# Products of the modulation vectors on VectorE alone and in a pinned order, and the out-projection's first input split at fixed places of the scan

## The chip, the core and the metric

The kernel runs on one core of a Trainium2 chip. The core's engines each work through their own list of instructions in order and wait for each other on semaphores: TensorE (PE: matmuls, with PEld for its weight loads), VectorE (DVE), ScalarE (ACT), GpSimd (POOL) and SyncE (SP), which here issues all the transfers (DMAs). The metric is the time of one execution in microseconds; lower is better.

## The reference, cut to what matters

A sequence of 1024 tokens of width 1024 runs through one Mamba-2 layer and one stick-breaking attention layer. A conditioning vector `c` gives shift, scale and gate vectors for each layer ("modulation"). All is float32.

```python
c_act = silu(c)
shift, scale, gate = split(c_act @ ada_w[0] + ada_b[0], 3)
h = rmsnorm(x) * (1 + scale) + shift
zxbcdt = h @ in_w                      # 2048 z, 2048 x, 4*128 B, 4*128 C, 32 dt
xbc = silu(causal_dwconv(xbc))         # 24 tiles of 128 channels, 4 taps each
y = chunked_scan(x, dt, B, C)          # 4 groups x 8 chunks of 128 tokens
y = group_rmsnorm((y + D * x) * silu(z))
x = x + gate * (y @ out_w)             # the out-projection
# shared K/V with its own shift and scale (c_act @ kv_ada_w), then attention
```

## The kernel before, in words

Every large matmul is made of three: weights and activations are split into a high and a low part, `hi = cast(v)` on ScalarE and `lo = v - hi` on VectorE, and the products hi·hi, hi·lo and lo·hi are summed (`mm3`, L128 to L131). All data are held with channels on the 128 partitions, and the sequence is worked in two halves of 512 tokens.

The program has these stages.

- **Start** (to about 77 us in the profile): input norm, the first two modulation vectors, the first three tiles of the x/B/C projection.
- **Projection and convolution** (77 to 313 us): 21 more tiles. For each, 48 matmuls fill a PSUM tile `pr` of 3 buffers; `conv` then does the first tap on ScalarE (L351) and three taps on VectorE (L353, tile `cv`), a SiLU on ScalarE, and a store to DRAM (`xs_d`, L357). The next tile's weights are split by L123 and L124 (`hx`, `lx`). After some tiles `ada_rest(i)` computes one of the six remaining modulation vectors: eight rows `ar` of 512 KB are loaded (3 buffers) and each is multiplied with the row `crow` and summed. Six of eight products are one VectorE instruction (L369); every fourth (`ADAP = 4`) is a GpSimd product (L366) and a summing pass on ScalarE (L367). The results are needed only by the out-projection and later.
- **Scan** (313 to 640 us): units i = 0 to 7, which are the 4 groups of the first half of the sequence and then of the second; four chunks of 128 tokens each. `chunk_a` loads and exponentiates the decay matrix `lm` (L509, GpSimd L515, ScalarE L518), transposes the chunk into `px` and `pb` (PE L523 to L526, from `xg`, `bt` and `ct`), and multiplies on VectorE (L529 to L539). `chunk_b` does the chunk's matmuls (`yd`, `yo`, `ps`, L550 to L565) and adds up (L562 to L573). `gate` (L575) multiplies with SiLU(z) and sums squares (`sq`: ScalarE L587 and L590, GpSimd L591); `norm_store` of a unit stands two chunks into the next unit and begins with the matmul `rs` of `sq` (L599). The matmuls of the next unit's z projection (`pz`) fill PE between these. PE's order in the scan is written by hand.
- **Out-projection** (from 599 us): `load_y(0)` brings the first half of the scan's output back from DRAM in 16 tiles `yr` (3 buffers, L662) and splits each (`yh` on ScalarE L663, `yl` on VectorE L664). These have no fixed place: outside a hand-written section a scheduler orders each engine's list by its own estimate. For the first half, matmuls `po` of the out-projection are also placed between the last chunks of the scan.
- K/V projection, attention and the last projection follow; nothing there is changed.

`tc.keep_in_program_order(i)` keeps an instruction at its place in the written program on its engine; without it the scheduler may move it ahead.

Of the kernel before, what the change touches and what calls it, by code (L numbers as in the profile page):

```python
# [12 lines left out]
F32 = mybir.dt.float32  # L13
F32R = mybir.dt.float32r
AF = mybir.ActivationFunctionType
ALU = mybir.AluOpType
# [3 lines left out]
P = 128  # L20
# [4 lines left out]
HT = T // NH  # L25
# [6 lines left out]
LAG = 3  # L32
AVD = 1
NPRE = 5
ADAP = 4

VEC = {}
_o = 0
# [9 lines left out]
def f(ap):  # L48
    return ap.bitcast(F32)
# [3 lines left out]
def tile_trunk(ctx, tc, xT, xN, c, vec, ada0, adar, wxbc, wwave, wdt, wz, wmo, wk, wv, wq, wqz, wso, out):  # L53
    nc = tc.nc
    V, S, Q, E, Y = nc.vector, nc.scalar, nc.gpsimd, nc.tensor, nc.sync

    def pool(es, name, bufs=1, **kw):
        return es.enter_context(tc.tile_pool(name=name, bufs=bufs, reuse_waits="tile", **kw))
# [11 lines left out]
    def vv(n, i=None, m=1):  # L70
        o, w = VEC[n]
        if i is None:
            return vt[:, o:o + w]
        return vt[:, o + i:o + i + m]
# [4 lines left out]
    ys_d = [[tc.dram_tile([4, P, HT], F32, name=f"ys_d{g}_{hf}") for hf in range(NH)] for g in range(G)]  # L79
# [14 lines left out]
    def weight_pools(es, n, nr, nw):  # L94
        wp["r"] = pool(es, f"wraw{n}", bufs=nr)
        wp["h"] = pool(es, f"whp{n}", bufs=nw)
        wp["l"] = pool(es, f"wlp{n}", bufs=nw)

    esw = ctx.enter_context(ExitStack())
    weight_pools(esw, 0, 2, 2)  # L100
    esy = esw.enter_context(ExitStack())
    pdt = pool(esy, "pdtv")

    dtv, wdv, acv, eev, nac = [pdt.tile([P, NC_, 32], F32, name=n)
# [5 lines left out]
    def act_tile(name):  # L110
        return act.tile([P, HT], F32R, tag="a", name=name)
# [46 lines left out]
    with ExitStack() as es:  # L158
        pp = pool(es, "pp1", bufs=3, space=PSUM)
        pcr = pool(es, "pcr")  # L160
        crow = pcr.tile([P, D], F32, name="crow")
# [198 lines left out]
        def ada_rest(i):  # L360
            dst = mod[:, (GA0, KSH, KSC, SH1, SC1, GA1)[i], :]
            for d in range(ND):
                r = pada.tile([P, D], F32, tag="ar", name=f"ar{i}_{d}", bufs=3)
                Y.dma_start(out=r, in_=adar[i, d])
                if d % ADAP == ADAP - 1:
                    Q.tensor_tensor(out=r, in0=r, in1=crow, op=ALU.mult)  # L366
                    S.activation(r, r, AF.Identity, accum_out=dst[:, d:d + 1])  # L367
                else:
                    V.scalar_tensor_tensor(out=r, in0=r, scalar=1.0, in1=crow, op0=ALU.mult,  # L369
                                           op1=ALU.mult, accum_out=dst[:, d:d + 1])  # L370
            bn, gn = ((GA0, "b_ga0", None), (KSH, "b_kvsh", None), (KSC, "b_kvsc", "gkv"),
                      (SH1, "b_sh1", None), (SC1, "b_sc1", "g1"), (GA1, "b_ga1", None))[i][1:]
            if gn is None:
                V.tensor_tensor(out=dst, in0=dst, in1=vv(bn), op=ALU.add)
            else:
                V.scalar_tensor_tensor(out=dst, in0=dst, scalar=1.0, in1=vv(bn), op0=ALU.add,
                                       op1=ALU.add)
                V.tensor_tensor(out=dst, in0=dst, in1=vv(gn), op=ALU.mult)
# [83 lines left out]

    pyr = pool(esy, "pyr", bufs=3)
    pxa = pool(esy, "pxa")
    with ExitStack() as es:
        ms = es.enter_context(ExitStack())
        ms.enter_context(tc.manual_schedule(engines={mybir.EngineType.PE}))
# [6 lines left out]
        def zproj(g, hf, j, dst):  # L476
            wh, wl = load_w(wz[4 * g + j], f"z{g}_{hf}_{j}")
            ps = mm_tile(f"pz{g}_{hf}_{j}")
            for k in range(ND):
                mm3(ps, wh[:, k, :], wl[:, k, :], *h0[k][hf], k == 0, k == ND - 1)  # L480
                if k == ND - 1:
                    S.copy(dst, ps)
                yield

        def load_g(g, hf):
            n = f"{g}_{hf}"
            hs = slice(hf * HT, (hf + 1) * HT)
            xg = pw.tile([P, 4, HT], F32, tag="xg", name="xg" + n)
            Y.dma_start(out=xg, in_=xs_d[g][0:4, :, hs].rearrange("j p t -> p j t"))
            bt = pq.tile([P, HT], F32, tag="bt", name="bt" + n, bufs=1)  # L490
            Y.dma_start(out=bt, in_=xs_d[g][4, :, hs])
            ct = pq.tile([P, HT], F32, tag="ct", name="ct" + n)
            Y.dma_start(out=ct, in_=xs_d[g][5, :, hs])
            sz = pw.tile([P, 4, HT], F32, tag="sz", name="sz" + n)
            y = py.tile([P, 4, HT], F32, tag="y", name="y" + n)
            return dict(g=g, hf=hf, xg=xg, bt=bt, ct=ct, sz=sz, y=y)
# [118 lines left out]
        for n, (i, cc) in enumerate(todo):  # L615
            u = units[i]
            c = u["hf"] * CPH + cc
            if cc == 0 and i + 1 < 2 * G:
                units.append(load_g((i + 1) % G, (i + 1) // G))
            z = iter(())  # L620
            if i + 1 < 2 * G:
                v = units[i + 1]
                z = zproj(v["g"], v["hf"], cc, v["sz"][:, cc, :])
            for _ in range(3):
                next(z, None)
            cur = stage
            if n + 1 < len(todo):
                i2, c2 = todo[n + 1]
                nxt = units[i2], units[i2]["hf"] * CPH + c2
                stage = chunk_a(*nxt)  # L630
            for _ in range(3):
                next(z, None)
            if cc == 2 and i > 0:
                norm_store(units[i - 1], sq)
            chunk_b(u, c, *cur)
            for _ in z:
                pass
            if cc == CPH - 1:
                sq = gate(u, n == len(todo) - 1)
        ms.close()  # L640
# [3 lines left out]
    with ExitStack() as es:  # L644
# [8 lines left out]
        def load_y(hf):  # L653
            hs = slice(hf * HT, (hf + 1) * HT)
            yy = []
            for k in range(16):
                mk = b_tile if hf == 1 and k < 8 else act_tile
                yy.append((mk(f"yh{k}_{hf}"), mk(f"yl{k}_{hf}")))
            for k in range(16):
                hi, lo = yy[k]  # L660
                r = pyr.tile([P, HT], F32, tag="yr", name=f"yr{k}_{hf}")
                Y.dma_start(out=r, in_=ys_d[k // 4][hf][k % 4])  # L662
                S.copy(hi, r)  # L663
                V.tensor_tensor(out=lo, in0=r, in1=f(hi), op=ALU.subtract)  # L664
            return yy
# [2 lines left out]
        hk = [[None] * NH for _ in range(ND)]  # L668
        h1 = [[None] * NH for _ in range(ND)]
        rb = [None] * NH  # L670
        ynext = load_y(0)
        for hf in range(NH):
            hs = slice(hf * HT, (hf + 1) * HT)
            yy = ynext
# [1 line left out]
            for d in range(ND):  # L676
# [4 lines left out]
                for kh in range(2):  # L681
                    wh, wl = load_w(wmo[kh, d], f"o{d}_{hf}_{kh}")
                    for k in range(8):
                        mm3(ps, wh[:, k, :], wl[:, k, :], *yy[kh * 8 + k], kh + k == 0, kh * 8 + k == 15)
                V.scalar_tensor_tensor(out=x1[d][hf], in0=ps, scalar=mod[:, GA0, d:d + 1], in1=xr,
                                       op0=ALU.mult, op1=ALU.add)
# [7 lines left out]
            if hf == 0:  # L694
                ynext = load_y(1)
# [16 lines left out]
        for hf in range(NH):  # L712
# [12 lines left out]
            for ch in range(2):  # L725
                ps = [pp.tile([P, 512], F32, tag=f"v{s}", name=f"pv{s}_{ch}_{hf}") for s in range(4)]
                for kp in range(4):
                    wh, wl = load_w(wv[ch, kp], f"v{kp}_{ch}_{hf}", (2, 512))
                    for kk in range(2):
                        k = kp * 2 + kk  # L730
# [222 lines left out]
    with ExitStack() as es:  # L953
# [25 lines left out]
        for hf, c0, c1, ds in ((1, 0, 512, (0, 5, 1, 2, 3, 4, 6, 7)), (0, 0, 256, (6, 7, 0, 1, 2, 3, 4, 5)),  # L979
# [55 lines left out]
            r = pf.tile(sh, F32, tag="rb", name="rb2_" + n)  # L1035
            inv_rms(pss, r, pf.tile(sh, F32, tag="sq", name="rt2_" + n), D)
            done = finish(hf, c0, c1, ds, x2, r)
        for eng, i0, i1 in ((V, 0, 2), (V, 2, 5), (V, 5, 8)):
            m = i1 - i0
            eng.tensor_tensor(out=x2t[:, i0:i1, :], in0=x2t[:, i0:i1, :],  # L1040
                              in1=r.unsqueeze(1).to_broadcast([P, m, w]), op=ALU.mult)
            Y.dma_start(out=out[ds[i0]:ds[i0] + m, :, c0:c1].rearrange("d p t -> p d t"),
                        in_=x2t[:, i0:i1, :])
# [68 lines left out]
```

## Time and profile before

| | |
|---|---|
| median of 3 runs | 1459.53 us (1458.59 to 1461.04) |
| the profiled execution, its own time | 1462.46 us |
| span of its instructions in the profile | 1460.8 us |
| PE busy | 1430.3 us, 98% of the span |
| VectorE, ScalarE, GpSimd busy | 962.0, 736.2, 516.5 us |
| mean granted TensorE clock | 0.994 of full speed |

Times in the profile count from the first instruction; the profiled execution took 1.7 us more than its span. A group of rows may give an engine's idle time and, after an arrow, the instruction or the transfer that ended it.

### The profile page before, as it was taken

To read this page: it belongs to the slowest core of one execution; us is meant where nothing else is said; L and a number is where in the kernel's file an instruction comes from. 1 tells how busy PE (TensorE), PEld (TensorE's weight loads), DVE (VectorE), ACT (ScalarE), POOL (GpSimd) and SP (SyncE) were. 2 spreads that over 40 slices of the span, in tenths; PEclk is the share of its full clock that TensorE was granted. 3 is DMA by queue.
4 is the path that set the end of the run, shared out by engine and by line. 5 is a ranking of instruction groups with operands and counts; after the bars stand their busy time and mean duration, and the time that the engine had idled before them with its cause. 6 is when DMAs were issued, how large, how long until landed. Compare 5 with 4: busy or idle time off the path is not lost.

```text
span 1460.8 us, 20961 instructions
## 1 busy us (share of the span) xinstructions
PE 1430.3 (98%) x7772; PEld 1125.7 (77%) x7772; DVE 962.0 (66%) x1211; ACT 736.2 (50%) x1236; POOL 516.5 (35%) x601
## 2 busy tenths in 40 slices
PE   7998999999999999999999999999999999999997
PEld 4777888887777777778888888887777777777797
DVE  5699975455788887975733627516666666667674
ACT  6654533246666666733532424335555555556452
POOL 0021220002555555531011000027666666667531
PEclk9999999999999999999999999999999999999999
DMA  9358875233577766667433546460222122212253
GB/s 368 129 202 318 295 285 182 101 107 132 183 236 220 234 217 217 195 201 266 151 123 128 182 144 227 159 211 31 80 69 70 59 73 63 68 58 81 92 183 116
DMA packets 105446, 235.76 MB, mean 161 GB/s; under 512 B 9344, under 2 KB 40832, under 8 KB 103296
## 3 DMA queue, kind: packets, MB, share of 16 engines
q1 hardware_dynamic: 105344, 234.42, 47.8%
q8 instruction: 61, 1.00, 0.3%
q14 instruction: 41, 0.34, 0.1%
HBM read 188.51 MB, written 45.88 MB: 160 GB/s over the span
## 4 chain that ended last, share of the span: by engine, by line
PE 90%; DVE 5%; ACT 2%; issue 1%; DMA 1%; POOL 0%; SPq 0%; DVEq 0%; ACTq 0%; POOLq 0%
PE av L891 5%; PE pr L129 5%; PE pr L130 5%; PE pr L131 5%; PE sc L838 4%; PE at L870 4%; PE pz L129 4%; PE pz L131 4%; PE pz L130 4%; PE po L131 4%; PE po L130 4%; PE po L129 4%; PE pq L129 2%; PE pqz L129 2%; PE yd L550 2%; PE pq L131 2%
## 5 line engine op out<-in xcount | busy, mean ns | idle before, releaser
L861 POOL TENSOR_TENSOR be<-be,kp 128x1024 f32<-128x1024 f32 (+2 forms) x96 | 163.3, 1702 | 82.6 <-DVE kp L855 73.6
L841 ACT ACTIVATE kp<-sc 128x1024 f32<-128x1024 f32 (+2 forms) x96 | 75.5, 813 | 149.2 <-PE sc L838 111.3
L855 DVE TENSOR_TENSOR_SCAN kp<-kp,pone 128x128 f32<-128x128 f32 (+3 forms) x128 | 96.7, 803 | 63.8 <-POOL kp L848 63.8
L129 PE MATMUL pr<-h0h,hx 128*128 128x512 f32 x336 | 131.7, 392 | 3.8 <-DVE cv L353 3.8
L131 PE MATMUL pr<-h0h,lx 128*128 128x512 f32 x336 | 131.5, 391 | 0.0
L130 PE MATMUL pr<-h0l,hx 128*128 128x512 f32 x336 | 131.5, 391 | 0.0
L129 PE MATMUL pz<-h0h,hz 128*128 128x512 f32 x256 | 113.0, 441 | 0.0
L130 PE MATMUL po<-yl,ho 128*128 128x512 f32 x256 | 100.9, 394 | 0.6 <-DVE yl L664 0.6
L131 PE MATMUL po<-yh,lo 128*128 128x512 f32 x256 | 100.0, 391 | 1.3 <-DVE lo L124 1.3
L131 PE MATMUL pz<-h0h,lz 128*128 128x512 f32 x256 | 100.4, 392 | 0.0
L130 PE MATMUL pz<-h0l,hz 128*128 128x512 f32 x256 | 100.0, 391 | 0.0
L129 PE MATMUL po<-yh,ho 128*128 128x512 f32 x256 | 100.0, 391 | 0.0
L366 POOL TENSOR_TENSOR ar<-ar,crow 128x1024 f32<-128x1024 f32 x12 | 31.1, 2596 | 182.4 <-DMA ar<-adar 163.0
L518 ACT ACTIVATE lm<-lm,nac 128x128 f32<-128x128 f32 x256 | 78.9, 390 | 31.8 <-POOL lm L515 31.8
L855 DVE TENSOR_TENSOR_SCAN kp<-kp,ab,pone 128x512 f32<-128x512 f32 x64 | 78.3, 1265 | 24.7 <-ACT kp L841 14.2
L124 POOL TENSOR_TENSOR lq<-rq,hq 128x256 fp32r<-128x256 f32 x32 | 22.5, 738 | 177.8 <-ACT hq L123 177.8
L515 POOL TENSOR_SCALAR_AFFINE_SELECT lm<-lm 128x1024 f32<-128x1024 f32 x32 | 42.1, 1316 | 118.3 <-DMA lm<-ac_d 108.9
L555 POOL TENSOR_TENSOR sd<-st,eev 128x512 f32<-128x512 f32 x24 | 37.5, 1561 | 126.1 <-ACT st L567 114.2
L353 DVE SCALAR_TENSOR_TENSOR cv<-pr,vt,cv 128x1023 f32<-128x1023 f32 (+2 forms) x63 | 80.2, 1276 | 0.9
L129 PEld LDWEIGHTS pr<-h0h,hx 128*128 128x128 f32 x336 | 63.5, 189 | 17.4 <-issue 4.2
L123 ACT CAST ho<-ro 128x1024 fp32r<-128x1024 f32 x32 | 33.6, 1052 | 84.5 <-PE po L130 74.3
L870 PEld LDWEIGHTS at<-ident,be 128*128 128x128 f32 x576 | 67.2, 140 | 10.6 <-DVE aT L880 0.9
(258 smaller groups left out, 3886.7 us busy)
## 6 DMA issues: line engine op xcount, KB each, us to landing
ar<-adar SPq DMA_DIRECT2D x48, 512.0 KB, 5.3
lm<-ac_d SPq DMA_DIRECT2D x32, 512.0 KB, 5.0
rz<-wz SPq DMA_DIRECT2D x32, 512.0 KB, 3.8
ro<-wmo SPq DMA_DIRECT2D x32, 512.0 KB, 3.7
xs_d<-sv SPq DMA_DIRECT2D x24, 512.0 KB, 4.1
rx<-wxbc SPq DMA_DIRECT2D x21, 512.0 KB, 4.6
a<-ada SPq DMA_DIRECT2D x8, 1024.0 KB, 10.1
xg<-xs_d SPq DMA_DIRECT2D x8, 1024.0 KB, 6.1
```

Source lines behind the costliest of these rows:

```text
L129: E.matmul(ps, wh, xh, start=first, stop=False)
L130: E.matmul(ps, wh, xl, start=False, stop=False)
L131: E.matmul(ps, wl, xh, start=False, stop=last)
L353: V.scalar_tensor_tensor(out=ac[:, i:], in0=ps[:, :T - i], scalar=vv("cw", m * 4 + 3 - i), in1=ac[:, i:], op0=ALU.mult, op1=ALU.add)
L515: Q.affine_select(out=lm, in_=lm, pattern=[[0, HPG], [1, P]], compare_op=ALU.is_ge, fill=-1e30, base=0, channel_multiplier=-1)
L518: e = S.activation(lm[:, h, :], lm[:, h, :], AF.Exp, bias=nac[:, c, h0_ + h:h0_ + h + 1])
L838: E.matmul(ps[:, a, o:o + w], q[hsl[a], x, i * P:(i + 1) * P], kd[hsl[a], y, HT * c:HT * c + w], start=b == 0, stop=b == 2)
L841: S.activation(kp[:, :, ok:ok + w], ps[:, :, o:o + w], AF.Sigmoid, scale=-0.125)
L855: V.tensor_tensor_scan(out=ka, data0=ka, data1=pone.to_broadcast([P, w]), initial=1.0 if top else above[p, i][:, a, 0:1], op0=ALU.mult, op ...
L861: Q.tensor_tensor(out=be[:, :, o:o + w], in0=be[:, :, o:o + w], in1=kp[:, :, ok + 1:ok + w + 1], op=ALU.mult)
L870: E.transpose(ps[:, j, :], be[:, a, j * P:(j + 1) * P], ident)
L891: E.matmul(ps[hsl[a], cs], vd[:, j, hsl[a]], at[j // 4][:, a, j % 4, cs], start=j == 0, stop=j == nj - 1)
```

## The change

The constant `ADAP` goes. All eight products of a modulation vector are VectorE instructions, and each is kept in program order, behind the taps of the tile that `ada_rest` follows. The pool of the `yr` tiles is made at the beginning of the program. The first half's loads and splits move from `load_y(0)` into the scan's loop: three loads after the first chunk of unit 4, then one split (with the load of the tile three further on) after each chunk of units 5 and 6 and two after each chunk of unit 7, casts and subtractions kept in program order.

```diff
@@ ada_rest
-                if d % ADAP == ADAP - 1:
-                    Q.tensor_tensor(out=r, in0=r, in1=crow, op=ALU.mult)
-                    S.activation(r, r, AF.Identity, accum_out=dst[:, d:d + 1])
-                else:
-                    V.scalar_tensor_tensor(out=r, in0=r, scalar=1.0, in1=crow, op0=ALU.mult,
+                v = V.scalar_tensor_tensor(out=r, in0=r, scalar=1.0, in1=crow, op0=ALU.mult,
                                            op1=ALU.mult, accum_out=dst[:, d:d + 1])
+                tc.keep_in_program_order(v)
@@ before the scan (the pool pyr moves up to the other pools of the first stages)
-    pyr = pool(esy, "pyr", bufs=3)
     pxa = pool(esy, "pxa")
+    y0, yraw = [], []
+
+    def y0_load(k):
+        r = pyr.tile([P, HT], F32, tag="yr", name=f"yr{k}_0")
+        Y.dma_start(out=r, in_=ys_d[k // 4][0][k % 4])
+        yraw.append(r)
+
+    def y0_split():
+        k = len(y0)
+        hi, lo = act_tile(f"yh{k}_0"), act_tile(f"yl{k}_0")
+        tc.keep_in_program_order(S.copy(hi, yraw[k]))
+        tc.keep_in_program_order(V.tensor_tensor(out=lo, in0=yraw[k], in1=f(hi), op=ALU.subtract))
+        y0.append((hi, lo))
+        if len(yraw) < 16:
+            y0_load(len(yraw))
@@ the scan's loop, after chunk_b and the rest of the z projection
+            if i == 4 and cc == 0:
+                for k in range(3):
+                    y0_load(k)
+            for _ in range(1 if i in (5, 6) else 2 if i == 7 else 0):
+                y0_split()
@@ the out-projection
-        ynext = load_y(0)
+        ynext = y0
```

How the lists move is shown at three places. First VectorE at the beginning of the convolutions. Before, with products `ar1_0` to `ar1_2` of the second modulation vector between the taps `cv` of the third, fourth and fifth tile (`dt..` are small steps of the step sizes):

```order
L414 TENSOR_SCALAR dtu_728<-dtu_728 128x256
L369 SCALAR_TENSOR_TENSOR ar1_0_1391,mod_126<-ar1_0_1391,crow_156 128x1024
L405 TENSOR_SCALAR dtq_734<-dte_731 128x256
L353 SCALAR_TENSOR_TENSOR cv2_795<-rw2_793,vt_67,cv2_795 128x1022
L369 SCALAR_TENSOR_TENSOR ar1_1_1394,mod_126<-ar1_1_1394,crow_156 128x1024
L374 TENSOR_TENSOR mod_126<-mod_126,vt_67 128x8
L353 SCALAR_TENSOR_TENSOR cv3_852<-pr3_803,vt_67,cv3_852 128x1022
L406 RECIPROCAL dtq_734<-dtq_734 128x256
L353 SCALAR_TENSOR_TENSOR cv2_795<-rw2_793,vt_67,cv2_795 128x1021
L124 TENSOR_TENSOR lx4_989<-rx4_986,hx4_988 128x1024
L369 SCALAR_TENSOR_TENSOR ar1_2_1397,mod_126<-ar1_2_1397,crow_156 128x1024
L353 SCALAR_TENSOR_TENSOR cv16_915<-pr16_866,vt_67,cv16_915 128x1023
```

The same place now:

```order
L411 TENSOR_SCALAR dtu_731<-dtu_731 128x256
L353 SCALAR_TENSOR_TENSOR cv2_798<-rw2_796,vt_67,cv2_798 128x1023
L402 TENSOR_SCALAR dtq_737<-dte_734 128x256
L124 TENSOR_TENSOR lx20_929<-rx20_926,hx20_928 128x1024
L353 SCALAR_TENSOR_TENSOR cv2_798<-rw2_796,vt_67,cv2_798 128x1022
L403 RECIPROCAL dtq_737<-dtq_737 128x256
L353 SCALAR_TENSOR_TENSOR cv3_855<-pr3_806,vt_67,cv3_855 128x1023
L353 SCALAR_TENSOR_TENSOR cv2_798<-rw2_796,vt_67,cv2_798 128x1021
L404 TENSOR_TENSOR dte_734<-dte_734,dtq_737 128x256
L353 SCALAR_TENSOR_TENSOR cv3_855<-pr3_806,vt_67,cv3_855 128x1022
L406 TENSOR_TENSOR dtz2_741<-dte_734 128x256
L353 SCALAR_TENSOR_TENSOR cv3_855<-pr3_806,vt_67,cv3_855 128x1021
```

No product stands there any more: the first one of all now stands six tiles later, behind the taps of `cv6`, and the products come in groups of eight after 6, 9, 12, 14, 16 and 18 of the 21 tiles, four or three of them ahead of the next tile's `lx`, the rest between the taps of the next one or two tiles.

Second SP at the loads of the scan's first chunk, `bt0_0`, `ct0_0` and `lm0_0`. Before, they stood between the store of the convolution's tile `sv8` and the weights `rx22`, in the middle of the convolutions:

```order
L357 DMA xs_d2_72<-sv8_1478 128x1024
L118 DMA rx22_1788<-wxbc 128x1024
L491 DMA bt0_0_2318<-xs_d0_70 128x512
L493 DMA ct0_0_2320<-xs_d0_70 128x512
L509 DMA lm0_0_2388<-ac_d_74 128x1024
L514 DMA eb0_0_2390<-ea_d_75 64x4x128 x2
```

Now:

```order
L118 DMA rz0_0_3_2439<-wz 128x1024
L118 DMA rz1_0_0_2479<-wz 128x1024
L357 DMA xs_d3_73<-sv23_2272 128x1024
L502 DMA bt0_0_2306<-xs_d0_70 128x512
L504 DMA ct0_0_2308<-xs_d0_70 128x512
L520 DMA lm0_0_2376<-ac_d_74 128x1024
L525 DMA eb0_0_2378<-ea_d_75 64x4x128 x2
```

They moved behind the store of the last of all the tiles, `sv23`. PE's place for the matmuls that read `bt0_0` and `ct0_0` (L525, L526) did not move.

Third VectorE at the beginning of the out-projection, the second and third chunk of the last unit (`xd3_5`, `lm3_5`: second chunk; `lo0_0_1`, `lo1_0_0`: weights of the out-projection). Before:

```order
L124 TENSOR_TENSOR lo0_0_1_5455<-ro0_0_1_5452,ho0_0_1_5454 128x1024
L573 TENSOR_TENSOR y2_1_4342<-yd2_7_5037,eb2_7_4902 128x4x128
L664 TENSOR_TENSOR yl11_0_5345<-yr11_0_5398,yh11_0_5344 128x512
L529 TENSOR_TENSOR xd3_5_5105<-px3_5_5097,dtv_145 128x512
L534 TENSOR_TENSOR xw3_5_5107<-px3_5_5097,wdv_146 128x512
L583 SCALAR_TENSOR_TENSOR y2_1_4342<-xg2_1_4335,vt_67,y2_1_4342 128x512 x4
L664 TENSOR_TENSOR yl12_0_5347<-yr12_0_5402,yh12_0_5346 128x512
L539 TENSOR_TENSOR lm3_5_5081<-pb3_5_5102,lm3_5_5081 128x1024
L664 TENSOR_TENSOR yl13_0_5349<-yr13_0_5406,yh13_0_5348 128x512
L124 TENSOR_TENSOR lo1_0_0_5491<-ro1_0_0_5488,ho1_0_0_5490 128x1024
```

Now:

```order
L124 TENSOR_TENSOR lo0_0_1_5443<-ro0_0_1_5440,ho0_0_1_5442 128x1024
L594 SCALAR_TENSOR_TENSOR y2_1_4336<-xg2_1_4329,vt_67,y2_1_4336 128x512 x4
L474 TENSOR_TENSOR yl7_0_5097<-yr7_0_4822,yh7_0_5096 128x512
L540 TENSOR_TENSOR xd3_5_5147<-px3_5_5139,dtv_148 128x512
L545 TENSOR_TENSOR xw3_5_5149<-px3_5_5139,wdv_149 128x512
L573 TENSOR_TENSOR eb3_4_5035<-yo3_4_5165,eb3_4_5035 128x512
L584 TENSOR_TENSOR y3_1_4733<-yd3_4_5154,eb3_4_5035 128x4x128
L550 TENSOR_TENSOR lm3_5_5123<-pb3_5_5144,lm3_5_5123 128x1024
L580 TENSOR_TENSOR st3_2303<-ps3_4_5171,sd3_4_5163 128x512
L474 TENSOR_TENSOR yl8_0_5176<-yr8_0_4912,yh8_0_5175 128x512
```

Fewer splits stand between the scan's own steps (the splits 0 to 6 are done long before). On PE, 18 matmuls `po` and the transposes of the second chunk now stand ahead of the first chunk's `yd` (31 before), and seven more and the third chunk's transposes between that chunk and the second chunk's `yd` (37 more before).

## Rows read from the trace of the kernel before

**Rows 1.** The page: span, and PE's busy time, share and instructions.

```profile
span 1460.8 us, 20961 instructions
PE 1430.3 (98%) x7772; PEld 1125.7 (77%) x7772; DVE 962.0 (66%) x1211; ACT 736.2 (50%) x1236; POOL 516.5 (35%) x601
```

**Rows 2.** Waits of PE: us in total, times, longest us.

```profile
PE pr L129 <- DVE cv L353: 3.8, 1, 3.8
...
PE rs L599 <- POOL sq L591: 2.8, 1, 2.8
...
PE po L131 <- DVE lo L124: 1.3, 1, 1.3
...
PE po L130 <- DVE yl L664: 0.6, 2, 0.3
```

**Rows 3.** Stretches: length, busy time by engine (instructions), PE clock, DMA share, GB/s.

```profile
114.70:118.10 3.40, 3.39 (x8) 2.73 (x9) 3.40 (x6) 2.99 (x3) 0.00 (x0) 0.50 0.97 371
...
127.30:138.00 10.70, 10.70 (x49) 8.87 (x48) 10.26 (x15) 3.89 (x4) 2.41 (x1) 1.00 1.02 372
...
473.10:476.50 3.40, 3.40 (x24) 3.07 (x24) 1.12 (x2) 2.49 (x9) 1.88 (x2) 0.50 0.73 248
```

**Rows 4.** Timeline of VectorE, convolutions: start, length, instruction, idle before.

```profile
77.19 1.22 DVE L369 SCALAR_TENSOR_TENSOR ar<-ar,crow 128x1024 f32<-128x1024 f32 x1
...
110.96 1.21 DVE L369 SCALAR_TENSOR_TENSOR ar<-ar,crow 128x1024 f32<-128x1024 f32 x1
...
112.10 2.46 DVE L353 SCALAR_TENSOR_TENSOR cv<-pr,vt,cv 128x1023 f32<-128x1023 f32 x2
```

**Rows 5.** Timeline of GpSimd, third unit of the scan.

```profile
470.68 1.26 POOL L591 TENSOR_TENSOR sq<-sq,sq 128x512 f32<-128x512 f32 x1 [3.16 <-ACT sq L590]
```

**Rows 6.** Timeline of ScalarE, third unit of the scan.

```profile
467.04 0.62 ACT L663 CAST yh<-yr 128x512 fp32r<-128x512 f32 x1 [5.05 <-DMA yr<-ys_d]
...
469.92 0.61 ACT L590 ACTIVATE sq<-y 128x512 f32<-128x512 f32 x1
```

**Rows 7.** Costs on VectorE, 60 to 330 us: count, busy us, mean ns.

```profile
L353 DVE SCALAR_TENSOR_TENSOR cv<-pr,vt,cv 128x1023 f32<-128x1023 f32 (+2 forms) x63 | 80.2, 1276 | 0.9
L369 DVE SCALAR_TENSOR_TENSOR ar<-ar,crow 128x1024 f32<-128x1024 f32 x36 | 47.0, 1309 | 5.6 <-DMA ar<-adar 5.6
```

**Rows 8.** Timeline of SP: the issue of transfers, convolutions' middle and end.

```profile
216.85 0.42 SPq L493 DMA_DIRECT2D ct<-xs_d x1
...
321.55 0.42 SPq L357 DMA_DIRECT2D xs_d<-sv x1
```

**Rows 9.** Timeline of PE: first chunk's transposes, out-projection's beginning.

```profile
324.85 0.39 PE L526 MATMUL pb<-ct,bt 128*128 128x128 f32 x2
...
599.28 0.39 PE L129 MATMUL po<-yh,ho 128*128 128x512 f32 x1
...
607.20 1.09 PE L550 MATMUL yd<-lm,xd 128*64 128x128 f32 x16
...
610.08 0.60 PE L523 MATMUL px<-ident,xg 128*128 128x128 f32 x4
```

**Rows 10.** Transfers issued from 216.4 to 216.9: KB each, us to landing.

```profile
bt<-xs_d SPq DMA_DIRECT2D x1, 256.0 KB, 2.7
ct<-xs_d SPq DMA_DIRECT2D x1, 256.0 KB, 6.0
```

**Rows 11.** Timeline of VectorE, last unit of the scan.

```profile
602.02 1.21 DVE L124 TENSOR_TENSOR lo<-ro,ho 128x1024 fp32r<-128x1024 f32 x1
...
606.14 4.76 DVE L583 SCALAR_TENSOR_TENSOR y<-xg,vt,y 128x512 f32<-128x512 f32 x4
...
612.53 1.21 DVE L539 TENSOR_TENSOR lm<-pb,lm 128x1024 f32<-128x1024 f32 x1
```

**Rows 12.** The page, transfers: number, KB each, median us to landing.

```profile
ar<-adar SPq DMA_DIRECT2D x48, 512.0 KB, 5.3
...
a<-ada SPq DMA_DIRECT2D x8, 1024.0 KB, 10.1
```

More of the change, by code (lines that the diff above doesn't have):

```diff
@@ L34 @@
 NPRE = 5
-ADAP = 4
 VEC = {}
@@ L101, in tile_trunk @@
     esy = esw.enter_context(ExitStack())
+    pyr = pool(esy, "pyr", bufs=3)
     pdt = pool(esy, "pdtv")
```

## The prediction, made before the changed kernel ran

> **What bounds the kernel now.** I read the page first, then PE's waits, then stretches around the longest waits, then the timelines of the engines that end them. The page gives PE 1430.3 of 1460.8 us [rows 1]; no other engine is near. So work taken off an engine is worth nothing by itself: only what PE waits for counts, and the list of PE's waits says where to look. Two waits stand out, each of them once: 3.8 us for `cv` and 2.8 us for `sq` [rows 2]. The out-projection's matmuls `po` have a longest wait of 1.3 for a weight's `lo`, and 0.6 in two for `yl` [rows 2]. The stretches show a second price: in the 3.40 us behind each of the two long waits the granted clock is 0.50, that is 1.2 instead of 2.4 GHz, with PE busy throughout [rows 3]. Matmuls of 3.4 us at half the clock are 1.7 us of work, so each of these two waits costs 1.7 us more.
>
> **Term 1, the products between the convolutions: gain 5.5 us.** The first wait ends at 114.70 [rows 3] and lasts 3.8 us, so PE wanted the `pr` buffer at 110.9. It was free when the two taps of `cv` had been done at 112.10 + 2.46 = 114.56, and VectorE was not idle before them: a product of 1.21 us stands immediately ahead [rows 4]. The order shows such products between all the taps here. In the trace VectorE runs from 76 to 115 us without a pause, and nine products stand in that stretch ahead of the taps, the first at 77.19 and the last at 110.96 [rows 4]. Without them, at 1.309 each [rows 7], the taps would end 11.8 us earlier, at about 102.8, some 8.1 us before PE wants the buffer. Not all of that can be had, since the first tap on ScalarE and PE's own matmuls set a floor for each tile, but half of 8 us can be used up and the wait is still gone. Gain 3.8 + 1.7 = 5.5 us.
>
> What is late next? The products come back six tiles later, and 12 more of them on VectorE. PE takes 10.70 us for 48 matmuls of a tile [rows 3]. VectorE's work for a tile is three taps of 1.276 and a subtraction of 1.21, together 5.0 [rows 4, 7, 11]; 12 more products of 1.309 [rows 7] are 15.7 us over a stage of more than 200, which lie under PE's 5.7 us of reserve in each tile. The groups of eight that follow tiles 14, 16 and 18 are the tight ones. In two tiles PE spends 21.4, VectorE 10.0 + 8 x 1.21 = 19.7. To that comes a wait: there are three `ar` buffers, the fourth row can be fetched only when the first product is done, and it lands 5.3 us after its issue [rows 12], so the fourth product waits about 5.3 - 2 x 1.21 = 2.9. That is 22.6, or 1.2 us late in a pair of tiles, 3.6 in all three, against the 8.1 of reserve. I cost it at nothing. If an `ar` row took the 10.1 us of the larger `a` rows [rows 12], the fourth product would wait 7.7 and the seventh some 2.5 more, 29.9 against 21.4, and this cover is gone (rival C).
>
> **Term 2, the splits in the third unit: gain 4.5 us.** The matmul `rs` waited 2.8 us for GpSimd's `sq`, which had itself waited 3.16 for ScalarE's `sq` [rows 2, 5]. ScalarE's timeline shows why that was late: at the head of its list stood the cast `yh` (L663), placed there by the scheduler, and ScalarE stood idle 5.05 us until the transfer of `yr` had landed; then it scaled `lm` and squared `sq` (0.61, from 469.92) [rows 6]. With the change no split stands ahead of unit 5, so the first half's casts can't be here, and `sq` can be done up to 5 us earlier, more than the 2.8 wanted. Gain 2.8 + 1.7 = 4.5 us. The splits now stand in units 5 to 7, their loads issued three splits ahead, and one cast and one subtraction of half a `lo`'s width (about 0.6 each by the 1.21 of [rows 11]) per chunk are covered by an engine with a third of its time idle [rows 1].
>
> **Term 3, the loads of the scan's first chunk: loss 5.2 us.** This is the part that the diff doesn't tell. `bt0_0` and `ct0_0` were issued at about 216 us, a hundred before their use [rows 8]; the order puts them behind the store of `sv23` on SP now. In the trace that store issues at 321.55 and takes 0.42 [rows 8]; `bt` then goes at 322.0 and `ct` at 322.4. The matmul that reads both starts at 324.85 and its place hasn't moved [rows 9]. How long the transfers take has two rows: issued together, 256 KB each, `bt` landed after 2.7 us and `ct` after 6.0 [rows 10]. They follow each other on the same queues again, so I take 6.0: `ct` lands at 328.4, PE waits 3.5 us. The order has nothing for PE to do ahead of it; the z projection's next matmuls stand behind. Waits of 2.8 and 3.8 both dropped the clock [rows 3], so this one does: + 1.7, together 5.2. Bounds: with 2.7 for `ct` the wait is 0.2 and the clock keeps; with the 10.1 us of a transfer four times the size [rows 12] it would be 7.6 + 1.7 = 9.3, which I call far-fetched for 256 KB. By the Trainium skill (DMA: Bandwidth & Descriptors, section "Anatomy of one DMA — SWDGE (gpsimd) path") a transfer takes about 2.0 us and its bytes at 436 GB/s; estimated from it, 256 KB land in 2.6 us, and the term would be 0.2 instead of 5.2. The trace's `bt` agrees with this, its `ct` with 6.0 does not. Behind the two on SP stand `lm0_0` and `eb0_0`, wanted only by the chunk's `yd`, later than the wait's end.
>
> **Term 4, the beginning of the out-projection: nothing.** Before, its matmuls wait 1.3 + 0.6 = 1.9 us. Now splits 0 to 6 are done early, so `yl` is no longer the reason; but fewer `po` stand ahead of the last unit's `yd`, so PE comes sooner and VectorE's `lm3_5` becomes the question. Before, PE needed 607.20 - 599.28 = 7.9 us for 31 `po` and a chunk's transposes (0.7, of which 0.60 for `px`): 0.23 a `po` [rows 9]. Now 18 of them and transposes are 4.9, the chunk's own matmuls 610.08 - 607.20 = 2.9, seven `po` and transposes 2.3: PE is at the second chunk's `yd` at 599.3 + 10.1 = 609.4. VectorE: the weights' `lo` from 602.02 to 603.2, then `y` four times in 4.76 at most (alone nearer 4 x 0.6 = 2.4), then `yl`, `xd`, `xw`, `eb`, `y` at 0.6 each and `lm` 1.21 [rows 11]: ready between 609.8 and 612.2, a wait of 0.4 to 2.8. The middle, 1.6, is as much as before's 1.9; I count 0, with bounds of -1.5 and +0.9, + 1.7 where the clock falls too.
>
> **The sum.** -5.5 - 4.5 + 5.2 + 0 = -4.8 us. The profiled execution took 1462.46 us, 1.7 more than its span and 2.9 more than the median; its span would become 1456.0. Taken off the median of 1459.53: **1454.7 us**.
>
> **Rivals.** *A, the first chunk's loads land in time:* both like `bt`, 2.7 us after issue [rows 10]. For it: nothing else has to be fetched at that point but weights. Against: `ct`'s 6.0. Then -10 + 0.2: 1449.7. (The Trainium skill's rule of term 3 is this rival's side.)
> *B, one gap stays or is replaced:* the convolutions' wait remains because ScalarE's first tap, not VectorE, becomes the last to come (5.5 not gained), or the out-projection's wait is at its upper bound with the clock (+2.6) and `ct` a bit later. For it: the waits look each like one late engine, but I removed them by chains worked out by hand. Then -4.8 with 2.6 to 5.5 added: 1457.3 to 1460.2, no difference that can be told.
> *C, VectorE becomes the bound of the convolutions:* from the point at which an `ar` row takes over some 8 us to land, the pinned products hold up the taps of the tiles behind them. By the 10.1 us above, 29.9 - 21.4 = 8.5 us late in each of three pairs of tiles, 25.5, less 8.1 of reserve: 17 us of waits. For it: in order, nothing can pass a product that waits for its row, where before GpSimd took a quarter of them; the DMA share is about 1.0 in this stage [rows 3]. Against: the page's median of 5.3. Then 1459.5 - 4.8 + 17: about 1472.
>
> **How the numbers follow.** My forecast has 0.55, A 0.15, B 0.18, C 0.12. The forecast's own range is 1450.5 to 1457.5 (term 3 smaller by the clock's 1.7 and term 4's -1.5 below; +0.9 and +1.7 above). For 8 in 10 the range takes in A, and B to its end: 1448.0 to 1460.5, which leaves C out. A measurement of this kernel can tell about 0.2%, 2.9 us. Faster by more than that: the forecast and A, less the part of the forecast near 1457, 0.68; within: B and that part, 0.20; slower: C, 0.12.
>
> **What the changed profile would show.** Term 1: no wait of PE for `cv` near 111 us and a granted clock of 1.00 there; else it is wrong, and the last of the chain tells whether ScalarE's tap took VectorE's place. Term 2: no `yh` in the third unit, and `rs` not in the list of waits. Term 3: a wait of `pb` for the transfer of `ct` or `bt` at about 320 to 325 us, some 3.5 us long and 3.4 us at 0.50 behind it; a wait below 1 us says rival A, and how long `ct` took from its issue says why. Term 4: waits for `lm` at the last unit's `yd`. Rival C would be waits of `pr` for `cv` in the second half of the convolutions with VectorE's products waiting for `ar`. The prediction is wrong most easily if the store of `sv23` comes earlier or later against PE than in the trace of before: half the loss hangs on 2 us there.

## The result, and the profile of the changed kernel

The changed kernel takes 1468.65 us (median of 4 runs, 1467.74 to 1472.94), the kernel before 1459.06 in the same comparison: a ratio of 1.0072, 95% interval 1.0047 to 1.0096 (the quotient of the two medians is 1.0066). It is slower by some 10 us, where 1454.7 was predicted. The profiled execution of the changed kernel took 1468.22 us. Its page begins with these lines, which answer to [rows 1]:

```profile
span 1466.3 us, 20942 instructions
PE 1431.1 (98%) x7772; PEld 1126.0 (77%) x7772; DVE 963.1 (66%) x1235; ACT 721.5 (49%) x1210; POOL 486.1 (33%) x589
```

GpSimd lost 30 us of work and ScalarE 15, VectorE gained 1. None of this is seen in the span, since PE bounds both kernels. PE's waits (us in total, times, longest), against [rows 2]:

```profile
PE po L130 <- DVE yl L474: 3.2, 1, 3.2
PE pb L536 <- DMA bt<-xs_d: 3.0, 1, 3.0
...
PE po L129 <- DVE x L701: 2.3, 1, 2.3
PE po L131 <- DVE lo L124: 2.0, 1, 2.0
...
PE pb L537 <- DMA ct<-xs_d: 0.7, 1, 0.7
```

Both waits that the prediction began with, for `cv` and for `sq`, are gone. Five others stand there: two for the first chunk's loads, three in the out-projection's beginning. Stretches of the changed kernel (length, busy time by engine, granted clock, DMA share, GB/s), against [rows 3]:

```profile
321.06:327.88 6.82, 6.14 (x15) 4.74 (x16) 0.14 (x1) 4.00 (x10) 1.84 (x2) 0.50 0.99 335
607.77:611.18 3.41, 3.07 (x18) 2.59 (x20) 3.38 (x6) 2.03 (x4) 1.52 (x2) 0.50 0.72 263
641.91:645.32 3.41, 3.41 (x9) 2.62 (x9) 2.52 (x2) 1.16 (x2) 1.99 (x2) 0.50 0.74 235
108.00:118.00 10.00, 10.00 (x45) 8.26 (x44) 6.69 (x9) 3.92 (x4) 0.00 (x0) 1.00 0.64 210
127.30:138.00 10.70, 10.70 (x49) 8.83 (x49) 4.79 (x5) 4.50 (x4) 0.00 (x0) 1.00 0.27 98
469.00:476.00 7.00, 7.00 (x44) 5.04 (x43) 6.51 (x9) 3.66 (x8) 0.42 (x2) 1.00 0.57 207
```

The clock is at half (1.2 GHz) behind each of the new groups of waits, and at full where it was at half before (115 and 473 us).

Where did the time go? Both kernels run the same matmuls, and the places used here stand in the same order in both, so the start of the same matmul in both timelines gives the lead. The scan's first transpose `px`: 324.30 before, 317.52 after, a lead of 6.8, of which 1.1 is already there at the first `pr` at 77 us, ahead of the wait for `cv`. A `px` two units later: 401.89 and 401.98, nothing left. The first `po`: 599.28 and 594.25, a lead of 5.0. The first `pk` of the K/V projection: 792.22 and 797.07, 4.8 behind. So four places, in this profile: the products -5.7, the first chunk's loads +6.9, the third unit -5.1, the beginning of the out-projection +9.9.

**The loads.** SP's timeline of the changed kernel and, below it, the transfers issued from 314 to 316 us (KB, us to landing), against [rows 8] and [rows 10]:

```profile
314.81 0.38 SPq L357 DMA_DIRECT2D xs_d<-sv  x1
315.28 0.38 SPq L502 DMA_DIRECT2D bt<-xs_d  x1
315.72 1.25 SPq L504 DMA_DIRECT2D ct<-xs_d  x1
```

```profile
bt<-xs_d SPq DMA_DIRECT2D x1, 256.0 KB, 5.7
ct<-xs_d SPq DMA_DIRECT2D x1, 256.0 KB, 6.5
```

PE's timeline there, against [rows 9]:

```profile
317.52 0.60 PE L534 MATMUL px<-ident,xg 128*128 128x128 f32 x4
321.07 0.48 PE L536 MATMUL pb<-ident,bt 128*128 128x128 f32 x1 [2.95 <-DMA bt<-xs_d]
322.22 0.80 PE L537 MATMUL pb<-ct,bt 128*128 128x128 f32 x2 [0.68 <-DMA ct<-xs_d]
```

The store `sv23` and PE come 6.7 and 6.8 us earlier, so their distance is that of before; `bt` lands at about 321.0, `ct` at 322.2. The waits are 3.6 together, and the 6.82 us at half the clock cost 3.4.

**The out-projection.** Two rows of VectorE, one of GpSimd and one of PE show its first wait, four of VectorE the other two:

```profile
600.12 4.58 DVE L594 SCALAR_TENSOR_TENSOR y<-xg,vt,y 128x512 f32<-128x512 f32 x4
604.63 1.75 DVE L474 TENSOR_TENSOR yl<-yr,yh 128x512 fp32r<-128x512 f32 x1
```

```profile
602.45 6.31 POOL L596 TENSOR_TENSOR y<-y,sz 128x512 f32<-128x512 f32 x4
```

```profile
606.43 0.51 PE L130 MATMUL po<-yl,ho 128*128 128x512 f32 x1 [3.23 <-DVE yl L474]
```

```profile
634.20 2.73 DVE L594 SCALAR_TENSOR_TENSOR y<-xg,vt,y 128x512 f32<-128x512 f32 x4
636.85 1.28 DVE L596 TENSOR_TENSOR y<-y,sz 128x512 f32<-128x512 f32 x2
638.06 0.74 DVE L701 SCALAR_TENSOR_TENSOR x<-po,mod,x 128x512 f32<-128x512 f32 x1
...
639.98 1.64 DVE L124 TENSOR_TENSOR lo<-ro,ho 128x1024 fp32r<-128x1024 f32 x1
```

The eighth split's subtraction `yl` stands on VectorE behind the four `y` of a gate (L594); its cast had begun at 595.65. The four `y` took 4.58 us and `yl` 1.75, while GpSimd was at work on its own part of the gate (L596); at 634 us four `y` take 2.73, and at 610.55 a `yl` 0.68. PE, which has come to that `po` at 603.2, waits for 3.2 us. Later PE has done all that it can with two PSUM tiles of `po` at 636.6; the first of them is read by `x` (L701), and that stands on VectorE behind the last unit's gate (L594, L596). Then the next weight's `lo` is late.

### The profile page after: what moved, and what is told of

It reads as the page before. It is cut to its first block, busy times and chain, and to the rows that moved or that the text cites. A ratio compares the mean times of both kernels' runs of the same rounds, so it can differ in the third digit from the quotient of the medians.

```text
span 1466.3 us, 20942 instructions
## 1 busy us (share of the span) xinstructions
PE 1431.1 (98%) x7772; PEld 1126.0 (77%) x7772; DVE 963.1 (66%) x1235; ACT 721.5 (49%) x1210; POOL 486.1 (33%) x589
## 4 chain that ended last, share of the span: by engine, by line
PE 91%; DVE 4%; DMA 2%; ACT 1%; issue 1%; SPq 0%; POOL 0%; DVEq 0%; ACTq 0%; POOLq 0%
PE pr L130 5%; PE pr L131 5%; PE pr L129 5%; PE av L907 5%; PE sc L854 4%; PE at L886 4%; PE pz L129 4%; PE pz L130 4%; PE pz L131 4%; PE po L131 4%; PE po L129 4%; PE po L130 4%; PE pq L129 2%; PE pqz L129 2%; PE pq L131 2%; PE yd L561 2%
## 5 line engine op out<-in xcount | busy, mean ns | idle before, releaser
L526 POOL TENSOR_SCALAR_AFFINE_SELECT lm<-lm 128x1024 f32<-128x1024 f32 x32 | 42.7, 1335 | 435.0 <-DMA lm<-ac_d 413.3
L886 PE MATMUL at<-ident,be 128*128 128x128 f32 x576 | 74.7, 272 | 0.5 <-DVE aT L896 0.5
L858 ACT ACTIVATE be<-sc 128x1024 f32<-128x1024 f32 x72 | 73.6, 1022 | 0.0
## 6 DMA issues: line engine op xcount, KB each, us to landing
a<-ada SPq DMA_DIRECT2D x8, 1024.0 KB, 10.1
```

Of the source, the lines that this page charges most:

```text
L858: S.activation(be, ps, AF.Sigmoid, scale=0.125)
L886: E.transpose(ps[:, j, :], be[:, a, j * P:(j + 1) * P], ident)
```

## The experiments

Each ratio is to runs of the kernel before on the same chip, with its 95% interval; it can differ from the quotient of the medians by up to 0.0012.

**1 to 4: the parts apart.** e1 has only the products changed (the diff's first part). e2 is the changed kernel with the products as before. In e3 and e4 one line moves:

```diff
@@ e3: the changed kernel, pool late      (e4: the kernel before, the same move the other way)
-    pyr = pool(esy, "pyr", bufs=3)        # ahead of the pool pdtv
     ...
+    pyr = pool(esy, "pyr", bufs=3)        # ahead of the pool pxa
```

Expected of e1: 

> The kernel before with only the products changed (all eight on VectorE, kept in program order); splits and pool as before. Theory S (the changed kernel's time is a sum of four places, read from the two traces: products -5.7, the first chunk's loads +6.9, the third unit -5.1, the beginning of the out-projection +9.8): only the first term is left, the wait at 111 us and its half clock are gone, so 5.7 below before, about 1453.5, and no wait for bt or ct at 318 us. Theory P (the products bring the losses too: in order on VectorE they push later work back, and the out-projection's wait is the end of that): at least half of the 9.8 shows here, the time is 1459 to 1464, and the trace has waits of po of over 5 us around 600 to 640 us.

Expected of e2: 

> The kernel after with the products as before (every fourth on GpSimd and ScalarE, not kept in order); pool and splits as in the changed kernel. Theory S: +6.9 - 5.1 + 9.8 = 11.6 above before, about 1470.7, with the wait for cv at 111 us back, the waits for bt and ct at about 325 us, and waits of po for yl, for x and for lo between 600 and 645 us. Theory P: the out-projection's 9.8 are gone, so about 1461.

Expected of e3: 

> The changed kernel with the pool of yr made where it was before; nothing else differs in the code. The order of SP then has bt0_0 and ct0_0 two stores of a convolution tile earlier. Theory S: the 3.0 and 0.7 us of waits for bt and ct and the half clock behind them are gone: 6.9 below the changed kernel, about 1461.8; the out-projection's waits stay. Rival W (the wait only moves, since the stores of the last tiles, lm and eb are now late instead): less than 2 us gained, 1467 to 1469, and the trace shows another wait of PE between 310 and 345 us.

Expected of e4: 

> The kernel before with one line moved: the pool of yr is made at the beginning, as in the changed kernel; products and splits as before. PE's order is that of before in every row, VectorE's differs in a few rows, SP's has bt0_0 and ct0_0 behind the store of the last tile. Theory S: the loads' term alone, +5.2 to +6.9, about 1465, with a wait of pb for bt or ct at about 325 us and half the clock behind it. If PE comes to these matmuls late enough (it is held at 111 us by the products here), the wait may be some 2 us shorter than the 3.7 of the changed kernel, never absent. Rival D (the place of the pool costs nothing by itself): about 1459.

| kernel | median us | ratio |
|---|---|---|
| e1, products alone | 1454.08 | 0.9961 (0.9948 to 0.9975) |
| e2, splits and pool | 1474.34 | 1.0088 (1.0065 to 1.0111) |
| e3, changed kernel, pool late | 1462.67 | 1.0013 (1.0002 to 1.0024) |
| e4, pool alone | 1466.28 | 1.0042 (1.0027 to 1.0057) |
| before, in these | 1459.70 | |

The sum holds. The products alone give 5.6. One line that makes a pool earlier costs 6.6, with no instruction of PE moved: e4's waits have the loads back,

```profile
PE pb L525 <- DMA bt<-xs_d: 2.9, 1, 2.9
```

and making the pool late again saves the changed kernel 6.0. What is left of the loss, e2 against e4, is 8.1 us and belongs to the splits. Theory P falls: e1 has the products and no loss. e2 came 3.6 above its expectation, which was made with the third unit's 5.1 in it (next).

**5: the kernel before, once more.** e1's profile lacked the third unit's wait, although its cast `yh` stands on ScalarE at the same place as before.

> The kernel before once more, unchanged, for a second profile. The first profiled execution took 1462.46 us, 3 above its median, and its wait of 2.8 us for sq in the third unit came behind a transfer of yr that took 8.4 us from issue to landing; with the products moved (e1) the same cast, at the same place in ScalarE's list, found its data after 5.3 us and PE did not wait. Theory V (that wait is an accident of one transfer in one execution, and the median never had it): no wait of rs for sq of over 0.5 us, no half clock at 470 to 480 us, and a span of about 1457. Theory T (the wait belongs to the kernel before, as the prediction took it): 2 to 3 us of wait again and a span of about 1461.

The second profile has a span of 1457.1 us (its execution 1458.83), against 1460.8. Its waits and its cast, against [rows 2] and [rows 6]:

```profile
PE pr L129 <- DVE cv L353: 3.2, 1, 3.2
...
PE rs L599 <- POOL sq L591: 0.5, 1, 0.5
```

```profile
465.62 0.62 ACT L663 CAST yh<-yr 128x512 fp32r<-128x512 f32 x1 [2.42 <-DMA yr<-ys_d]
```

The transfer that the cast waits for took 6.0 us to land here, 5.3 in e1, and in the first profile of before:

```profile
yr<-ys_d SPq DMA_DIRECT2D x1, 256.0 KB, 8.4
```

With 6.0 PE waits 0.5 us and the clock stays at 1.00; with 8.4 it waits 2.8 and loses 1.7 more. Theory V holds for this wait: it was one slow transfer in the one execution that was profiled. No other profile with the cast at this place (e1 and e4 above, e6, e10 and e11 below) has more than 0.5 us of it.

The place is not empty for that. In the second profile PE also waits there for `lm`:

```profile
460.81 1.09 PE L550 MATMUL yd<-lm,xd 128*64 128x128 f32 x16 [1.45 <-DVE lm L539]
```

From the first `px` of the third unit to the first of the fifth, PE takes 79.1 us in the first profile of before (401.89 to 480.98), 76.6 in the second (401.34 to 477.96), 74.8 in e1 (396.18 to 471.00) and 74.0 in the changed kernel (401.98 to 475.96). So moving the splits away from here saves 0.8 to 2.6 us where that transfer isn't slow, and not 5.1; what of it the median has is not shown.

The wait for `cv` at 111 us came again (3.2), with its half clock. Against this second profile the changed kernel's span is 9.2 longer, which is what the medians say (9.6).

**6 to 9: the out-projection.** All four are e3 (pool late) with one thing different in the splits. The kernel before took 1459.11 us beside e6 to e8 and 1459.76 beside e9 to e11.

```diff
@@ e6: splits free
-        tc.keep_in_program_order(S.copy(hi, yraw[k]))
-        tc.keep_in_program_order(V.tensor_tensor(out=lo, in0=yraw[k], in1=f(hi), op=ALU.subtract))
+        S.copy(hi, yraw[k])
+        V.tensor_tensor(out=lo, in0=yraw[k], in1=f(hi), op=ALU.subtract)
@@ e7: eight fixed; load_y(0, 8) makes the other eight in the out-projection
-            for _ in range(1 if i in (5, 6) else 2 if i == 7 else 0):
+            for _ in range(2 if i == 5 else 0):
@@ e8: the first eight earlier
+            for _ in range(2 if i in (5, 7) else 0):
@@ e9: the last eight earlier
+            for _ in range(1 if i in (5, 6) else 4 if i == 7 and cc < 2 else 0):
```

Expected of e6: 

> The changed kernel with the pool of yr made late, as in e3, and the splits not kept in program order (the loads and the splits are written in the scan as before). PE's list is then that of the kernel before, with 31, 68, 72 and 105 matmuls po ahead of the last unit's four yd, where e3 has 18, 25, 55 and 74. Theory O (the out-projection's 8 to 10 us come from the list that the fixed splits bring with them: PE comes to the last unit's chunks too early, and VectorE's x and lo are left behind the last gate): all of it comes back, 1454 as e1, with no wait for x. Rival L (the loss is in the scan's loads of yr, which stand in SP's list ahead of lm and eb): at most half comes back, 1458 to 1462.

Expected of e7: 

> As e3, but only the first eight splits are fixed, two after each chunk of unit 5; the other eight are loaded and split in the out-projection's own code, free as before. PE's list is that of the kernel before again (31, 68, 72, 105). Theory O: about 1454, like e1, whatever the first eight do. Theory T (a wait in the third unit is saved by late splits): 4 to 5 us less than e1, about 1449. Rival F (fixing any splits costs): 1458 or more.

Expected of e8: 

> As e3, all sixteen splits fixed, but the first eight after the chunks of unit 5 (two each) and none in unit 6, so that the eighth, for whose yh PE waited 1.8 us in e3 (3.2 us for yl in the changed kernel), is long done at 594 us; the last eight as in e3. PE's list has 15, 25, 54 and 74 po ahead of the four yd. Rival Y (the eighth split's lateness is the out-projection's loss): 3.5 us less than e3 with the clock, about 1459. Theory O: less than 2 us gained, since the waits for x and lo at the list's end, and PE's early arrival at the chunks, stay: 1461 to 1464.

Expected of e9: 

> As e3, all sixteen splits fixed, the first eight one after each chunk of units 5 and 6, but the last eight four after the first and four after the second chunk of unit 7 instead of two after each. PE's list has 18, 25, 56 and 90 po ahead of the last unit's four yd and 170 ahead of its last rs, as many as the kernel before there (e3: 18, 25, 55, 74 and 122). Theory O, that the loss lies in what is left for after the scan's last chunk: the waits for x and lo at 636 to 640 us go, 3 to 6 us less than e3, so 1457 to 1460; the 1.8 for yh at about 600 stays. Rival Q (the loss is made at the first two chunks, by 18 and 25 po where there were 31 and 68): less than 2 us gained, 1461 to 1463.

| kernel | `po` ahead of the last unit's four `yd` | median us | ratio |
|---|---|---|---|
| e3 | 18, 25, 55, 74 | 1462.67 | 1.0013 (1.0002 to 1.0024) |
| e6, splits free | 31, 68, 72, 105 | 1452.33 | 0.9954 (0.9939 to 0.9969) |
| e7, eight fixed | 31, 68, 72, 105 | 1455.89 | 0.9978 (0.9968 to 0.9988) |
| e8, first eight earlier | 15, 25, 55, 74 | 1462.71 | 1.0025 (1.0016 to 1.0035) |
| e9, last eight earlier | 18, 25, 61, 90 | 1457.11 | 0.9974 (0.9963 to 0.9986) |

The counts are those of the traces; the third ones that were expected for e8 and e9 (54 and 56) end at the `rs` ahead of that `yd`.

e6 gets all of it back: with the splits free, the list of PE is the old one, and so are its waits at the out-projection's beginning (0.3 for `yl`, 1.3 for `lo`). It does not decide rival L, though, because the loads of `yr` went back with the splits: the fourth one is issued at 437 us in e6 and at 438 in e1, at 532 in e3.

e8 takes away the 1.8 us for `yh`, and the time is that of e3. This does not decide rival Y, for e8 brought waits of the same size: the splits, now two after each chunk of unit 5, delay `y`, for which `yd` then waits 1.0 and 1.8 us at 559 and 570 us, and 1.1 at 605. The waits at the end of the scan stay.

```profile
PE yd L561 <- DVE y L584: 3.9, 3, 1.8
...
PE po L128 <- DVE x L701: 2.3, 1, 2.3
...
PE po L130 <- DVE lo L123: 2.2, 2, 2.0
```

Nor was the 1.8 us of e3 the eighth split's, as the expectation of e8 has it. It is the 25th `po` that waits, the first one of the ninth split, whose cast stands on ScalarE behind the next chunk's `lm` (in e8 behind three of its eight parts only, at 601.37):

```profile
600.94 2.45 ACT L529 ACTIVATE lm<-lm,nac 128x128 f32<-128x128 f32 x8 [3.38 <-POOL lm L526]
603.29 0.24 ACT L549 COPY bs<-pb 128x128 f32<-128x128 f32 x1
603.44 0.61 ACT L473 CAST yh<-yr 128x512 fp32r<-128x512 f32 x1
```

```profile
604.11 0.50 PE L128 MATMUL po<-yh,ho 128*128 128x512 f32 x1 [1.84 <-ACT yh L473]
```

e9 leaves the first half of the list alone and changes its end: 5.6 us come back, more than half of the loss, and rival Q falls. From 531 to 606 us its loads of `yr` are issued within 1 us of e3's, so this part isn't theirs, against rival L. In e9 VectorE takes `x` ahead of the gate, and PE's waits for `x` are gone:

```profile
630.44 0.74 DVE L701 SCALAR_TENSOR_TENSOR x<-po,mod,x 128x512 f32<-128x512 f32 x1
633.56 0.74 DVE L701 SCALAR_TENSOR_TENSOR x<-po,mod,x 128x512 f32<-128x512 f32 x1
634.22 2.73 DVE L594 SCALAR_TENSOR_TENSOR y<-xg,vt,y 128x512 f32<-128x512 f32 x4
```

What e9 still lacks to e6, 4.8 us, is not separated; its profile has 1.8 for the ninth split's `yh`, 1.5 for transposes and 1.2 for a weight of the z projection.

e7 has the old list of PE with half of the splits fixed. It came 1.9 above the 1454 expected of theory O, and 3.6 above e6. In its profile PE waits for `y` at 557 and 568 us, 2.8 together, behind the last of the fixed splits on VectorE: a fixed split can cost where it stands ahead of something that PE waits for, even when PE's list doesn't change. But the profiled execution (1453.08) was the shortest of the ten and only 1.3 above that of e6, so most of the 3.6 is not explained. Theory T's 1449 did not come: between the two `px` named above, e7 takes 74.0 us and e6 74.8, so 0.8 was to be saved there.

**10 and 11: which half of the products' edit.** e10 is the kernel before with its VectorE products kept in order and every fourth still on GpSimd; e11 has all eight on VectorE, none kept in order.

Expected of e10: 

> The kernel before with its six VectorE products of eight kept in program order; every fourth stays on GpSimd and ScalarE; pool and splits as before. No product then stands between the first six tiles' taps on VectorE. Theory K (term 1 comes from the order alone): as e1, 5.6 below before, about 1454, no wait for cv at 111 us. Rival M (it needs the products off GpSimd and ScalarE as well, because a GpSimd product makes VectorE's subtraction beside it 2.2 us longer): 1457 or more.

Expected of e11: 

> The kernel before with all eight products on VectorE and none kept in order; pool and splits as before. Products stand between the first tiles' taps as before, one or two more of them than before. Theory K: the wait for cv at 111 us stays or grows by the 1.2 us of each added product, less the 2.2 us that a subtraction beside a GpSimd product took longer: 1458 to 1461, no gain. Rival M: at least half of the 5.6 us shows, 1454 to 1457.

e10: 1454.21 us, 0.9954 (0.9938 to 0.9970). e11: 1454.01, 0.9953 (0.9935 to 0.9972). Neither has a wait for `cv`. Each half alone gives the whole gain, so theory K, order alone, is wrong, and so is its rival as far as it asked for both. e11 still has twelve products between 77 and 113 us. What it doesn't have is GpSimd's products. (ScalarE's summing passes went with them; but VectorE was busy from 76 to 115 us in the kernel before, so they are not what held its taps.) In the kernel before, a row of GpSimd and one of VectorE beside it:

```profile
106.64 3.31 POOL L366 TENSOR_TENSOR ar<-ar,crow 128x1024 f32<-128x1024 f32 x1 [6.82 <-DVE dtq L406]
```

```profile
107.61 3.42 DVE L124 TENSOR_TENSOR lx<-rx,hx 128x1024 fp32r<-128x1024 f32 x1
```

and the same subtraction in e11:

```profile
104.70 1.16 DVE L124 TENSOR_TENSOR lx<-rx,hx 128x1024 fp32r<-128x1024 f32 x1
```

The subtraction ended 1.08 us after GpSimd's product (111.03 and 109.95), as if it had only then begun; that this is what happens is not shown. Three VectorE instructions were stretched so ahead of the late taps, by about 2.2 us each, one beside each of GpSimd's three products there: this one, a product of 3.43 at 83.0 and a small step of 2.39 (0.28 in e11) at 97.6. Together 6.5 us, more than the 3.8 that PE waited. The Trainium skill (GPSIMD Engine Reference, section "1. Specifications") says that GpSimd shares its interfaces to SBUF with VectorE, and that VectorE's instructions with two SBUF inputs contend. The trace agrees for this one (`rx` and `hx` are both in SBUF): 3.42 beside a GpSimd product, 1.16 without.

## Why the prediction was wrong

**Term 1, predicted -5.5, measured -5.6 (e1).** The place, the price and the clock's share were right. Its cause was half of the truth: the products in front of the taps and the stretching beside GpSimd made the wait together, and taking away either is enough (e10, e11). Rival C did not come: the `ar` rows land in 4.8 us (5.3 before), and no `pr` waits.

**Term 2, predicted -4.5, measured -0.8 (against e1), -2.6 (against e5) and -5.1 (against the first profile).** That the place is better without the splits was right. Most of the size was not: the step that failed here is the last of the sum, "Taken off the median". I had noted that the profiled execution stood 2.9 us above the median and then subtracted from the median a wait that belonged to the excess. The profile had shown that this wait hung on one transfer.

**Term 3, predicted +5.2, measured +6.9 in the profile and +6.6 (e4).** The mechanism was right: the order put the loads behind `sv23`, and PE waited 3.6 us, by my 3.5. That it was for `bt` as well (5.7 us to landing, where I took 2.7) made no difference, since `ct` came last (6.5, I took 6.0). The size was off by the clock: half speed lasted 6.8 us behind this wait in the changed kernel and in e4, not 3.40; behind the same wait in e2's profile it lasted 3.4. Rival A is refuted. So is the 2.6 us for 256 KB as an estimate of these two transfers: the Trainium skill (DMA: Bandwidth & Descriptors, section "Anatomy of one DMA — SWDGE (gpsimd) path") gives its rule for transfers that GpSimd issues. These were issued by SyncE, directly behind a store; for one issued by GpSimd no run here shows it. What moved the loads was the pool's line, which the prediction did not single out.

**Term 4, predicted 0, measured +9.9 in the profile.** This is the step that failed and turned the sign. I followed PE and VectorE from the first `po` to the second chunk's `yd`, found PE there 10.1 us behind the first `po` with a wait of 0.4 to 2.8, and closed the account. PE came to it after 15.6 us (594.25 to 609.84), and the wait there was 0.3. The price lay on both sides of that place. Ahead of it, at the eighth split, 3.2 and a half clock: `yl` was in my chain of VectorE, but I asked only when `lm` would be ready, not when PE wants `yl`. And I let VectorE keep its distance to PE: the `lo` that opens the chain ended 3.9 us behind the first `po` before and 6.0 now, and `yl` took 1.75 us where I took 0.6. Behind it, at 636 to 642 us, 2.3 and 2.0 and a half clock again: fewer `po` ahead of the scan's steps (18, 25, 55, 74) means that more of them are left for after the last chunk, when VectorE is in the last gate. My bounds for the term (+0.9, with the clock +2.6) were made from the one place that I had looked at.

The runs price terms 2 and 4 only together: the splits, predicted at -4.5, cost 8.1 (e2 against e4). With the parts as measured, -5.6 + 6.6 + 8.1 is +9.1 us; the change measured +9.6. A slip in the prediction's range makes no difference to this: the terms that it names put the forecast's lower end at 1451.5, not 1450.5.

The parts can be separated with profit. e6, the products and the splits' code but the pool late and the splits free, takes 1452.33 us: 0.46% faster than before (0.31 to 0.61%) and some 16 us faster than the changed kernel. e1, e10 and e11 are within 2 us of it, so what the splits' code adds to the products is not told apart from nothing.

## What to carry to other kernels

An instruction that is fixed in the order moves others: a scheduler that fills the rest by its own estimate rebuilds the list of the engine that bounds the kernel, so read that list to the end of the stage and ask at each place what is in front on the engine it waits for. Before a wait is put into the sum, ask whether the median has it: a wait behind a single transfer in one profile, in an execution that stands above the median, wants a second profile. And a line that only creates a buffer earlier can move loads by a hundred microseconds in the queue; compare the transfers' order first.

## What was not expected of the hardware

- A VectorE subtraction beside a GpSimd product ended 1.08 us after it, 3.42 us long where it takes 1.16 to 1.23 alone. The other two stretched instructions ended 1.08 and 0.15 us after theirs.
- How long the granted clock was at 0.50 differed between executions for the same waits. Behind 2.9 to 3.0 us for `bt` and 0.2 to 0.7 for `ct` it was 6.8 us in the changed kernel and in e4, 3.4 in e2; behind 2.3 for `x` and 2.0 for `lo`, 3.4 in the changed kernel and in e8, 6.8 in e3.
- Even whether it fell differed: behind 0.3 us for `yl` and 1.3 for `lo` at the out-projection's beginning it was at 0.50 for 3.4 us in e1 and e10, and stayed at 1.00 in e5, e6 and e11.
- The same 256 KB transfer, with the same transfers ahead of it, landed in 5.3, 6.0 and 8.4 us in three executions; only behind the longest did PE wait for `sq` for over 0.5 us.
- Two profiles of one kernel differed by 3.7 us in span (1460.8 and 1457.1), 2.5 of it between the first `px` of the third unit and that of the fifth.
